# Where token operands begin in SBUF relative to the split weights: one encoder layer in fp32 pieces on one core

## The chip, the cores and the metric

The kernel runs on one NeuronCore of a Trainium2 chip. The metric is the device time of one execution in microseconds (us). The time before is the median of three runs; beside it stands one execution that was taken with the hardware profiler, whose rows are shown further down.

## The reference

One layer over 256 tokens of width 2048, in float32. What matters here are its matrix products: each takes all tokens against a large weight matrix.

```python
h = rmsnorm(x, norm_mix_pre[l])
z = h @ w_in[l]                                  # 2048 x 13312
conv_b, conv_c, conv_in, q, k, v, g_a, g_b = jnp.split(z, IN_OFFSETS, axis=-1)
y_a = short_conv_mixer(conv_b, conv_c, conv_in, conv_w[l], w_out_conv[l])   # ... @ w_out
...
y_b = block_gqa(q, k, v) @ w_out_attn[l]
...
mixed = (gate_a * y_a + gate_b * y_b) @ w_merge[l]
x = x + rmsnorm(mixed, norm_mix_post[l])
h = rmsnorm(x, norm_mlp_pre[l])
f = jnp.square(jax.nn.relu(h @ w_up[l])) @ w_down[l]
x = x + rmsnorm(f, norm_mlp_post[l])
```

## The kernel before

**Split products.** Every fp32 operand is split into a high and a low float32r part (`split`: ScalarE writes `hi`, VectorE writes `lo = src - hi`), and each product is three matmuls: high x high, high x low, low x high.

**Weights.** A projection is one block of 512 output columns by 2048 inputs. Its weights come by DMA into `raw`, 128 x 1024 at a time, and are split into `whi` and `wlo` (lines 75 and 76). One such pair of tiles is called a granule here: 256 of the 2048 inputs, so a projection has 8 granules. `weights` takes the tiles of the granules from a ring of four in the pool `wts`; once the mixing part is over (line 486) a second ring of four, `wts2`, is there, and granules then go four to `wts`, four to `wts2`, in turn (line 123). A projection after that point therefore has four granules of either ring, `wts` first.

**Two kinds of projection.**
- `linear_channels` (lines 161 to 200): the weights are stationary (loaded into the array, 128 columns at a time) and the tokens move, 256 columns each. 24 matmuls a granule, from lines 175, 179 and 182. Used by the convolution's three inputs (12 projections), both gates (8), `w_oc` (4), `w_oa` (4) and `w_up` except its first (15): 43 projections.
- `linear` (lines 133 to 159): the tokens are stationary and the weights move, 512 columns each. 12 matmuls a granule, from lines 145 to 147. Used by K, V and Q (6 projections), `w_mg` (4), the first of `w_up` (1) and `w_dn` (16): 27 projections.

**Token operands** are made by `pair`: 128 partitions x (2, 16, 256) float32r, the high parts in the first half. Three tags, each one place: A holds `hT` (the normalised input; it moves for the convolution and the gates and is stationary for K, V, Q), later `xr`, later `fT` (the hidden layer, stationary for `w_dn`); B holds `yT` (moves for `w_oc`), then `mT` (stationary for `w_mg`), later `facc`; C holds `oT` (moves for `w_oa`), then `x2T` (moves for `w_up`, stationary for its first projection).

**Places.** Pools lie one behind the other in each partition in the order in which they are opened (lines 61 to 65, then `mx`, in whose place `wts2` and `late` are opened later), and each tile takes a multiple of 32 bytes. The tiles of `big`, `wts` and `wk` are all multiples of 256 bytes, so where `big` begins decides where all of them begin modulo 256. The small tiles of `sm` lie between `wk` and what follows.

**Order.** The three matmuls of a step follow each other without a pause; `later` and `tick` put the attention's and the convolution's small work between granules by a fixed count.

Of the kernel before, what the change touches and what calls it, by code (L numbers as in the profile page):

```python
# [9 lines left out]
F32 = mybir.dt.float32  # L10
F32R = mybir.dt.float32r
# [4 lines left out]
P = 128  # L16
D = 2048
T = 256
NT = T // P
KT = D // P  # L20
# [12 lines left out]
def trunk_kernel(  # L33
# [16 lines left out]
    nc = tc.nc  # L50
# [8 lines left out]
    WARM = 9  # L59

    const = ctx.enter_context(tc.tile_pool(name="const", bufs=1))
    big = ctx.enter_context(tc.tile_pool(name="big", bufs=1))
    wts = ctx.enter_context(tc.tile_pool(name="wts", bufs=WB))
    wk = ctx.enter_context(tc.tile_pool(name="wk", bufs=2))
    sm = ctx.enter_context(tc.tile_pool(name="sm", bufs=2))
    ps_acc = ctx.enter_context(tc.tile_pool(name="ps_acc", bufs=4, space=bass.MemoryType.PSUM))
    ps_tr = ctx.enter_context(tc.tile_pool(name="ps_tr", bufs=2, space=bass.MemoryType.PSUM))
    ps_at = ctx.enter_context(tc.tile_pool(name="ps_at", bufs=2, space=bass.MemoryType.PSUM))
# [11 lines left out]
                lo, src, scale, hi.bitcast(F32), op0=ALU.mult, op1=ALU.subtract  # L80
            )

    def pair(tag):

        both = big.tile([P, 2, KT, T], F32R, tag=tag, name=tag)
        return both[:, 0], both[:, 1], both

# [43 lines left out]
    def linear(act, wv, done, k0=0, k1=KT, lag=0, ahead=None):  # L133

        ah, al, _ = act
        accs = [ps_acc.tile([P, CH], F32, name="acc") for _ in range(NT)]

        def step(t, k, wh, wl):  # L140
            ts_ = slice(t * P, (t + 1) * P)
            for g in range(KG):
                a = k - k0 + g
                first, last = a == 0, a == k1 - k0 - 1
                nc.tensor.matmul(accs[t], lhsT=ah[:, a, ts_], rhs=wh[:, g, :], start=first, stop=False)  # L145
                nc.tensor.matmul(accs[t], lhsT=ah[:, a, ts_], rhs=wl[:, g, :], start=False, stop=False)  # L146
                nc.tensor.matmul(accs[t], lhsT=al[:, a, ts_], rhs=wh[:, g, :], start=False, stop=last)  # L147
            if k + KG == k1:
                done(t, accs[t])

        behind = []
        for gran in weights(wv, k0, k1, ahead):
            behind.append(gran)
            step(0, *gran)
            if len(behind) > lag:
                step(1, *behind.pop(0))
            tick()
        for gran in behind:
            step(1, *gran)

    def linear_channels(act, wv, done):

        ah, al, _ = act
        accs = [ps_acc.tile([P, 2, T], F32, name="acc") for _ in range(CH // P // 2)]

        def step(c, k, wh, wl):
            cs = slice(c * P, (c + 1) * P)  # L170
            acc = accs[c // 2][:, c % 2, :]
            for g in range(KG):
                a = k + g

                nc.tensor.matmul(  # L175
                    acc, lhsT=wh[:, g, cs], rhs=ah[:, a, :], start=a == 0 and c % 2 == 0, stop=False,
                    skip_group_check=True,
                )
                nc.tensor.matmul(  # L179
                    acc, lhsT=wh[:, g, cs], rhs=al[:, a, :], start=False, stop=False, skip_group_check=True  # L180
                )
                nc.tensor.matmul(  # L182
                    acc, lhsT=wl[:, g, cs], rhs=ah[:, a, :], start=False, stop=a == KT - 1, skip_group_check=True
                )


        end = []
        for gran in weights(wv, 0, KT):
            if gran[0] >= KT - END * KG:
                end.append(gran)  # L190
            else:
                for c in range(CH // P):
                    step(c, *gran)
                tick()
        for c in range(0, CH // P, 2):
            for gran in end:
                step(c, *gran)
                step(c + 1, *gran)
            done(c, accs[c // 2])
            tick(END // 2)  # L200
# [57 lines left out]
        nc.scalar.activation(act, zero[:, :1], AF.Square)  # L258
    ident = const.tile([P, P], F32, name="ident")
    make_identity(nc, ident)  # L260
    mhalf = const.tile([P, 1], F32, name="mhalf")
    nc.vector.memset(mhalf, -0.5)
    ch = const.tile([P, 7, KT], F32, name="ch")
    nc.scalar.dma_start(ch, chan)
    g_pre, g_mlp, cw = ch[:, 0, :], ch[:, 1, :], ch[:, 2:5, :]
    g_bias = ch[:, 5:7, :]

    hT = pair("A")

    def first_operands(k, n):  # L270
        xt = mx.tile([P, KA, T], F32, tag="rope", bufs=4, name="xt")
# [1 line left out]
        for i in range(n):  # L273
            split(xt[:, i, :], hT[0][:, k + i, :], hT[1][:, k + i, :], scale=g_pre[:, k + i : k + i + 1])

    rstd = const.tile([P, NT], F32, name="rstd")
    norm_row = wk.tile([P, 2, T], F32, name="bias", bufs=1)
    xv = x.rearrange("(t p) d -> p t d", p=P)
    tabs = [mx.tile([P, 2, NT, HD], F32, name=f"tab{i}", bufs=1) for i in range(2)]

    def norm_in():

        ss0 = const.tile([P, NT, 4], F32, name="ss0")
        for j in range(4):
            xj = mx.tile([P, NT, CH], F32, tag="t4", bufs=4, name="xj")
            nc.sync.dma_start(xj, xv[:, :, j * CH : (j + 1) * CH])
            for t in range(NT):
                row_squares(ss0[:, t, j : j + 1], xj[:, t, :])
        total(rstd, ss0)
        along_rows(norm_row[:, 0, :], [rstd[:, t : t + 1] for t in range(NT)])  # L290
        nc.vector.tensor_tensor(norm_row[:, 1, :], norm_row[:, 0, :], norm_row[:, 0, :], op=ALU.mult)
# [78 lines left out]
        hT, w_in[C_V], lambda t, acc: split(acc, vh[:, t, :], vl[:, t, :], scale=rstd[:, t : t + 1])  # L370
    )

    oT = pair("C")
    yT = pair("B")

    def mm3(acc, a, b, first, last):
        nc.tensor.matmul(acc, lhsT=a[0], rhs=b[0], start=first, stop=False)  # L377
# [3 lines left out]
    def attention(j):  # L381
# [5 lines left out]
        def scores(hp, t, prob):  # L387
            ts_ = slice(t * P, (t + 1) * P)
            sc = ps_at.tile([P, 2, T], F32, name="at")
            for i in range(2):  # L390
                mm3(sc[:, i, :], (qh[:, hp + i, ts_], ql[:, hp + i, ts_]), (kh[:, j, :], kl[:, j, :]), True, True)
            nmax = sm.tile([P, 2], F32, name="nmax")
            nc.vector.tensor_reduce(nmax, sc, axis=AX.X, op=ALU.max, negate=True)
            pr = mx.tile([P, 2, T], F32, name="pr")
            den = sm.tile([P, 2], F32, name="den")
            for i in range(2):
                nc.scalar.activation(
                    pr[:, i, :], sc[:, i, :], AF.Exp, bias=nmax[:, i : i + 1], accum_out=den[:, i : i + 1]
                )
            rden = sm.tile([P, 2], F32, name="rden")  # L400
            nc.vector.reciprocal(rden, den)
            for i in range(2):
                nc.vector.tensor_scalar_mul(pr[:, i, :], pr[:, i, :], rden[:, i : i + 1])
            prob.append(pr)
# [102 lines left out]
    for j in range(4):  # L507
# [4 lines left out]
                nc.vector.tensor_tensor(m[:, j * 4 + c : j * 4 + c + 2, :], acc, g[:, c : c + 2, :], op=ALU.mult)  # L512

        linear_channels(yT, w_oc[j], done)
    mT = pair("B")
    for j in range(4):
        g = gate(C_GB, j, 1)
        def done(c, acc):
# [14 lines left out]
    rows1 = const.tile([P, 6], F32, name="rows1")  # L533

    def row_rsqrt(parts, t, at):
        s = sm.tile([P, 1], F32, name="s1")
        nc.vector.tensor_reduce(s, parts[:, t, :], axis=AX.X, op=ALU.add)
        r = rows1[:, at : at + 1]
        rsqrt_mean(r, s, D)
        return r  # L540


    ss1 = const.tile([P, NT, 4], F32, name="ss1")
    ss2 = const.tile([P, NT, 4], F32, name="ss2")
    xr = big.tile([P, 2, NT, D], F32, tag="A", name="xr")[:, 0]
    nc.scalar.dma_start(xr, xv)
    x2T = pair("C")
    rstd2 = [None] * NT
    mgs = []

# [79 lines left out]
    before = [None] * NT  # L630

    def finish(t, last):
        ms = sm.tile([P, 1], F32, name="ms3")
        nc.vector.scalar_tensor_tensor(ms, ss3[:, t, 3:4], 1.0 / D, before[t], op0=ALU.mult, op1=ALU.add)
        r = sm.tile([P, 1], F32, name="rs3")
        nc.gpsimd.tensor_tensor(r, ms, mhalf, op=ALU.pow)
        for c in range(4):
            js = slice(c * CH, (c + 1) * CH)
            f = facc[:, t, js] if c < 3 else last
            nc.vector.scalar_tensor_tensor(x2[:, t, js], f, r, x2[:, t, js], op0=ALU.mult, op1=ALU.add)  # L640
            nc.sync.dma_start(outv[:, t, js], x2[:, t, js])

    def down(q, j, fT):
        js = slice(j * CH, (j + 1) * CH)
        g = gain_row(4 + j) if q == 3 else None

        def done(t, acc):
            fj = facc[:, t, js]
            if q == 0:
                nc.scalar.copy(fj, acc)  # L650
                return
            nc.vector.tensor_tensor(fj, acc, fj, op=ALU.add)
            if q < 3:
                return
            row_squares(ss3[:, t, j : j + 1], fj)
            if j < 3:
                nc.vector.tensor_tensor(fj, fj, g, op=ALU.mult)
            else:
                last = wk.tile([P, CH], F32, tag="cc", bufs=CCB, name="cc")
                nc.vector.tensor_tensor(last, fj, g, op=ALU.mult)  # L660
                finish(t, last)
            if j == 2:
                s = sm.tile([P, 1], F32, name="s1")
                nc.vector.tensor_reduce(s, ss3[:, t, :3], axis=AX.X, op=ALU.add)
                before[t] = rows1[:, 4 + t : 5 + t]
                nc.vector.tensor_scalar(before[t], s, 1.0 / D, EPS, op0=ALU.mult, op1=ALU.add)

        linear(fT, w_dn[j], done, q * KT, (q + 1) * KT, lag=LAG if q == 3 and j == 3 else 0)

    for q in range(4):  # L670
        fT = pair("A")
        for j in range(4):
            if q == 0 and j == 0:
                hidden(q, j, fT)
# [65 lines left out]
```

## Time and profile before

| | |
|---|---|
| median of three runs | 1626.02 us (1625.46 to 1627.36) |
| the profiled execution | 1625.61 us |
| its span, first to last instruction | 1623.8 us |
| PE busy with matmuls | 1610.9 us, 99% of the span, 11210 instructions |
| weight loads (PEld) | 1497.9 us, 92% |
| VectorE, ScalarE, GpSimd busy | 947.5 us (58%), 709.5 us (44%), 35.6 us (2%) |
| DMA | 306.28 MB, mean 189 GB/s |

Busy time of PE counts matmuls that overlap in the pipeline, so how fast they follow each other is read from their starts, or from how many stand in a stretch of time. The span lacks the 1.8 us of the execution that lie around it.

### The profile page before, as it was taken

How to read it: one execution, taken by the hardware profiler on the slowest of the kernel's cores; microseconds unless marked ns; L12 is line 12 of the kernel's file. 1: busy time of each engine (PE TensorE's matmuls, PEld its weight loads, DVE VectorE, ACT ScalarE, POOL GpSimd, SP SyncE). 2: the span in 40 equal slices, each digit the busy share in tenths (PEclk: the TensorE clock that was granted, in tenths of full speed). 3: DMA queues.
4: the chain of work that ended last, by engine and by line, in shares of the span. 5: the costliest groups of instructions: out<-in, count | busy, mean ns of one | idle time of the engine just before them, and what ended most of it. 6: DMA issues, size and time to landing. Idle time of an engine off the chain costs nothing.

```text
span 1623.8 us, 26863 instructions
## 1 busy us (share of the span) xinstructions
PE 1610.9 (99%) x11210; PEld 1497.9 (92%) x11210; DVE 947.5 (58%) x1107; ACT 709.5 (44%) x860; POOL 35.6 (2%) x23
## 2 busy tenths in 40 slices
PE   9999999999999999999999999999999999999997
PEld 7899999999999999999988898889988998899986
DVE  6767676576764544555554865446654565555654
ACT  7444444444454443444444644444433344333441
POOL 0210101001000000000000000000000000000000
PEclk9999999999999999999999999999999999999999
DMA  8654545555475556565765566555565565556562
GB/s 317 204 177 156 181 147 181 181 167 183 149 241 186 186 188 194 186 190 184 243 204 177 172 209 195 189 187 189 185 197 189 187 190 189 193 182 195 191 200 83
DMA packets 86297, 306.28 MB, mean 189 GB/s; under 512 B 9632, under 2 KB 10016, under 8 KB 85920
## 3 DMA queue, kind: packets, MB, share of 16 engines
q1 hardware_dynamic: 84608, 300.32, 57.2%
q10 hardware_dynamic: 1568, 4.25, 0.8%
q8 instruction: 87, 1.43, 0.4%
q14 instruction: 34, 0.28, 0.1%
HBM read 302.44 MB, written 2.10 MB: 188 GB/s over the span
## 4 chain that ended last, share of the span: by engine, by line
PE 97%; DVE 1%; issue 1%; DMA 0%; POOL 0%; ACT 0%; SPq 0%; DVEq 0%; POOLq 0%; ACTq 0%
PE acc L182 20%; PE acc L175 20%; PE acc L179 20%; PE acc L146 12%; PE acc L147 12%; PE acc L145 12%; PE at L377 0%; PE at L379 0%; PE at L378 0%; PE tr L410 0%; DMA raw<-in_w_in 0%; PE tr L224 0%; POOL rs L236 0%; DVE wlo L76 0%; PE tr L575 0%
## 5 line engine op out<-in xcount | busy, mean ns | idle before, releaser
L76 DVE TENSOR_TENSOR wlo<-raw,whi 128x1024 fp32r<-128x1024 f32 (+1 forms) x561 | 684.2, 1221 | 602.8 <-ACT whi L75 590.9
L75 ACT CAST whi<-raw 128x1024 fp32r<-128x1024 f32 (+1 forms) x561 | 587.1, 1048 | 774.2 <-PE acc L179 401.6
L175 PE MATMUL acc<-A,whi 128*128 128x256 f32 x1280 | 362.3, 283 | 0.0
L182 PE MATMUL acc<-A,wlo 128*128 128x256 f32 x1280 | 360.4, 282 | 0.0
L179 PE MATMUL acc<-A,whi 128*128 128x256 f32 x1280 | 360.3, 282 | 0.0
L175 PE MATMUL acc<-C,whi 128*128 128x256 f32 x1216 | 340.0, 280 | 0.0
L182 PE MATMUL acc<-C,wlo 128*128 128x256 f32 x1216 | 339.9, 280 | 0.0
L179 PE MATMUL acc<-C,whi 128*128 128x256 f32 x1216 | 339.9, 279 | 0.0
L145 PE MATMUL acc<-whi,A 128*128 128x512 f32 x704 | 275.0, 392 | 2.2 <-ACT whi L75 2.2
L146 PE MATMUL acc<-wlo,A 128*128 128x512 f32 x704 | 275.9, 392 | 1.0 <-DVE wlo L76 1.0
L147 PE MATMUL acc<-whi,A 128*128 128x512 f32 x704 | 275.3, 391 | 0.0
L179 PEld LDWEIGHTS acc<-A,whi 128*128 128x128 f32 x1280 | 244.4, 191 | 0.2
L175 PEld LDWEIGHTS acc<-A,whi 128*128 128x128 f32 x1280 | 244.4, 191 | 0.2
L182 PEld LDWEIGHTS acc<-A,wlo 128*128 128x128 f32 x1280 | 244.5, 191 | 0.0
L175 PEld LDWEIGHTS acc<-C,whi 128*128 128x128 f32 x1216 | 230.8, 190 | 0.2
L179 PEld LDWEIGHTS acc<-C,whi 128*128 128x128 f32 x1216 | 230.8, 190 | 0.2
L182 PEld LDWEIGHTS acc<-C,wlo 128*128 128x128 f32 x1216 | 230.8, 190 | 0.0
L145 PEld LDWEIGHTS acc<-whi,A 128*128 128x128 f32 x704 | 131.8, 188 | 32.1 <-ACT whi L75 3.1
L146 PEld LDWEIGHTS acc<-wlo,A 128*128 128x128 f32 x704 | 132.0, 187 | 31.9 <-DVE wlo L76 2.7
L147 PEld LDWEIGHTS acc<-whi,A 128*128 128x128 f32 x704 | 132.0, 187 | 29.0
L182 PE MATMUL acc<-B,wlo 128*128 128x256 f32 x256 | 71.6, 280 | 0.0
L179 PE MATMUL acc<-B,whi 128*128 128x256 f32 x256 | 71.6, 280 | 0.0
(144 smaller groups left out, 1115.6 us busy)
## 6 DMA issues: line engine op xcount, KB each, us to landing
raw<-in_w_in SPq DMA_DIRECT2D x207, 512.0 KB, 4.3
raw<-in_w_up SPq DMA_DIRECT2D x128, 512.0 KB, 3.5
raw<-in_w_dn SPq DMA_DIRECT2D x128, 512.0 KB, 3.4
raw<-in_w_oc SPq DMA_DIRECT2D x32, 512.0 KB, 4.4
raw<-in_w_oa SPq DMA_DIRECT2D x32, 512.0 KB, 4.3
raw<-in_w_mg SPq DMA_DIRECT2D x32, 512.0 KB, 4.1
xj<-in_x SPq DMA_DIRECT2D x4, 512.0 KB, 9.0
xr<-in_x ACTq DMA_DIRECT2D x1, 2048.0 KB, 9.7
```

The lines of the kernel that those rows point to most:

```text
L75: nc.scalar.copy(hi, src)
L76: nc.vector.tensor_tensor(lo, src, hi.bitcast(F32), op=ALU.subtract)
L145: nc.tensor.matmul(accs[t], lhsT=ah[:, a, ts_], rhs=wh[:, g, :], start=first, stop=False)
L146: nc.tensor.matmul(accs[t], lhsT=ah[:, a, ts_], rhs=wl[:, g, :], start=False, stop=False)
L147: nc.tensor.matmul(accs[t], lhsT=al[:, a, ts_], rhs=wh[:, g, :], start=False, stop=last)
L175: nc.tensor.matmul(acc, lhsT=wh[:, g, cs], rhs=ah[:, a, :], start=a == 0 and c % 2 == 0, stop=False, skip_group_check=True,)
L179: nc.tensor.matmul(acc, lhsT=wh[:, g, cs], rhs=al[:, a, :], start=False, stop=False, skip_group_check=True)
L182: nc.tensor.matmul(acc, lhsT=wl[:, g, cs], rhs=ah[:, a, :], start=False, stop=a == KT - 1, skip_group_check=True)
```

## The change

The order of the instructions on every engine stays as it was, and so do their shapes; no matmul, copy or DMA is added or taken away. What changes is where tiles begin.

- The pool `sm` is opened directly behind `const`, ahead of `big`.
- Small tiles are put together or share a place (`ss0` and `ss1` in `ss01`; `mhalf` and `rstd` in `half`; `nmax` and `den` in `tops`; three late tiles take the tags of earlier ones). The memset of `mhalf` becomes one of 128 x 4.
- `pair` is told whether the tokens move or are stationary, and takes its part of a slightly longer tile: A is 64 bytes longer and begins 64 bytes in where tokens move; B is 192 bytes longer and begins 192 bytes in where they are stationary; C stays.

```diff
     const = ctx.enter_context(tc.tile_pool(name="const", bufs=1))
+
+    sm = ctx.enter_context(tc.tile_pool(name="sm", bufs=2))
     big = ctx.enter_context(tc.tile_pool(name="big", bufs=1))
     wts = ctx.enter_context(tc.tile_pool(name="wts", bufs=WB))
     wk = ctx.enter_context(tc.tile_pool(name="wk", bufs=2))
-    sm = ctx.enter_context(tc.tile_pool(name="sm", bufs=2))
...
-    def pair(tag):
-
-        both = big.tile([P, 2, KT, T], F32R, tag=tag, name=tag)
-        return both[:, 0], both[:, 1], both
+
+
+    LATE = {"A": {True: 16, False: 0}, "B": {True: 0, False: 48}, "C": {True: 0}}
+
+    def pair(tag, moving):
+
+        n, at = 2 * KT * T, LATE[tag][moving]
+        flat = big.tile([P, n + max(LATE[tag].values())], F32R, tag=tag, name=tag)
+        both = flat[:, at : at + n].rearrange("p (h k t) -> p h k t", h=2, k=KT)
+        return both[:, 0], both[:, 1]
...
-    mhalf = const.tile([P, 1], F32, name="mhalf")
-    nc.vector.memset(mhalf, -0.5)
+    ss01 = const.tile([P, 2, NT, 4], F32, name="ss01")
+    half = const.tile([P, 4], F32, name="half")
+    nc.vector.memset(half, -0.5)
+    mhalf = half[:, :1]
+    rstd = half[:, 2:4]
...
-    hT = pair("A")
+    hT = pair("A", True)
...
-    oT = pair("C")
-    yT = pair("B")
+    oT = pair("C", True)
+    yT = pair("B", True)
...
-    mT = pair("B")
+    mT = pair("B", False)
...
-    x2T = pair("C")
+    x2T = pair("C", True)
...
-        fT = pair("A")
+        fT = pair("A", False)
```

The byte at which the operands of the large products begin in each partition, and that byte modulo 256, as the two programs are built:

| tile | before | modulo 256 | after | modulo 256 |
|---|---|---|---|---|
| `wts` ring, first `whi` (the others at steps of 4096) | 148768 | 32 | 149440 | 192 |
| `wts2` ring, first `whi` (the others at steps of 4096) | 190432 | 224 | 190400 | 192 |
| A, moving (`hT`) | 17696 | 32 | 18176 | 0 |
| A, stationary (`fT`) | 17696 | 32 | 18112 | 192 |
| B, moving (`yT`) | 99616 | 32 | 100096 | 0 |
| B, stationary (`mT`) | 99616 | 32 | 100288 | 192 |
| C (`oT`, `x2T`) | 66848 | 32 | 67328 | 0 |
| `kv` (attention) | 50464 | 32 | 50944 | 0 |
| `qh`, `ph` (attention) | 212960, 190432 | 224 | 212928, 190400 | 192 |

## Rows read from the trace of the kernel before

**Rows 1.** The page: span and the engines' busy time.

```profile
span 1623.8 us, 26863 instructions
PE 1610.9 (99%) x11210; PEld 1497.9 (92%) x11210; DVE 947.5 (58%) x1107; ACT 709.5 (44%) x860; POOL 35.6 (2%) x23
```

**Rows 2.** The page: the chain that ended last, shares of the span by engine.

```profile
PE 97%; DVE 1%; issue 1%; DMA 0%; POOL 0%; ACT 0%; SPq 0%; DVEq 0%; POOLq 0%; ACTq 0%
```

**Rows 3.** Waits of PE, longest first: total us, times, longest us.

```profile
PE acc L145 <- ACT whi L75: 2.2, 2, 1.5
PE tr L256 <- DVE mhalf L262: 1.1, 1, 1.1
```

**Rows 4.** Windows of one w_up projection's two halves; counts include matmuls reaching in.

```profile
core 0: us, PE busy (x) PEld busy (x) DVE busy (x) ACT busy (x) POOL busy (x), PEclk, DMA share, GB/s
...
1103.66:1115.18 11.52, 11.52 (x98) 11.52 (x97) 8.16 (x9) 4.92 (x6) 0.00 (x0) 1.00 0.56 176
1115.18:1126.06 10.88, 10.88 (x98) 10.88 (x97) 5.21 (x6) 4.38 (x5) 0.00 (x0) 1.00 0.58 193
```

**Rows 5.** Timeline of PE where a w_up projection changes rings: start us, us.

```profile
1092.54 0.28 PE L179 MATMUL acc<-C,whi 128*128 128x256 f32 x1
1092.66 0.28 PE L182 MATMUL acc<-C,wlo 128*128 128x256 f32 x1
1092.78 0.28 PE L175 MATMUL acc<-C,whi 128*128 128x256 f32 x1
...
1093.12 0.28 PE L175 MATMUL acc<-C,whi 128*128 128x256 f32 x1
```

**Rows 6.** Windows of one w_dn projection's two halves.

```profile
1192.97:1203.87 10.90, 10.90 (x49) 9.01 (x48) 5.84 (x6) 4.21 (x4) 0.00 (x0) 1.00 0.60 194
1203.87:1215.07 11.20, 11.20 (x49) 8.98 (x48) 5.20 (x5) 4.19 (x4) 0.00 (x0) 1.00 0.58 187
```

**Rows 7.** Lines 182 and 145: ns min/median/max, first and last start.

```profile
L182 PEld LDWEIGHTS acc<-A,wlo x1280: 187/192/193, 76.7 to 786.6; 128*128 128x128 f32 x183
L182 PE MATMUL acc<-A,wlo x1280: 276/283/285, 76.8 to 786.7; 128*128 128x256 f32 x183
L182 PEld LDWEIGHTS acc<-C,wlo x1216: 187/188/192, 652.5 to 1526.6; 128*128 128x128 f32 x174
L182 PE MATMUL acc<-C,wlo x1216: 276/278/287, 652.6 to 1526.7; 128*128 128x256 f32 x174
...
L145 PE MATMUL acc<-whi,A x704: 388/389/507, 4.9 to 1614.6; 128*128 128x512 f32 x176
...
L145 PE MATMUL acc<-whi,B x128: 388/394/398, 809.2 to 899.0; 128*128 128x512 f32 x128
```

**Rows 8.** Line 378, the attention's products: scores, then values.

```profile
L378 PEld LDWEIGHTS at<-kv,qh x32: 187/188/188, 103.4 to 422.3; 128*128 128x128 f32 x32
L378 PE MATMUL at<-kv,qh x32: 276/276/276, 103.5 to 422.4; 128*128 128x256 f32 x32
L378 PEld LDWEIGHTS at<-pl,kv x32: 187/190/192, 116.7 to 436.1; 128*128 128x128 f32 x32
L378 PE MATMUL at<-pl,kv x32: 276/279/283, 116.8 to 436.2; 128*128 128x256 f32 x32
```

**Rows 9.** Timeline of PE in the convolution, ring wts alone.

```profile
190.55 0.28 PE L179 MATMUL acc<-A,whi 128*128 128x256 f32 x1
...
191.50 0.28 PE L175 MATMUL acc<-A,whi 128*128 128x256 f32 x1
```

**Rows 10.** Window of Q projection granules, ring wts, and of a convolution with attention.

```profile
62.12:67.56 5.44, 5.44 (x26) 4.50 (x24) 3.12 (x3) 2.11 (x2) 0.00 (x0) 1.00 0.88 315
130.00:140.00 10.00, 10.00 (x87) 10.00 (x86) 10.00 (x20) 4.16 (x6) 0.00 (x0) 1.00 0.29 91
```

**Rows 11.** Timeline there: a granule's low part on DVE.

```profile
134.24 1.22 DVE L76 TENSOR_TENSOR wlo<-raw,whi 128x1024 fp32r<-128x1024 f32 x1
```

**Rows 12.** Timeline there: PE's first use of that low part.

```profile
136.09 0.28 PE L182 MATMUL acc<-A,wlo 128*128 128x256 f32 x1
```

More of the change, by code (lines that the diff above doesn't have):

```diff
@@ L133, in linear @@
     def linear(act, wv, done, k0=0, k1=KT, lag=0, ahead=None):
-        ah, al, _ = act
+        ah, al = act
         accs = [ps_acc.tile([P, CH], F32, name="acc") for _ in range(NT)]
@@ L161, in linear_channels @@
     def linear_channels(act, wv, done):
-        ah, al, _ = act
+        ah, al = act
         accs = [ps_acc.tile([P, 2, T], F32, name="acc") for _ in range(CH // P // 2)]
@@ L274, in first_operands @@
             split(xt[:, i, :], hT[0][:, k + i, :], hT[1][:, k + i, :], scale=g_pre[:, k + i : k + i + 1])
-    rstd = const.tile([P, NT], F32, name="rstd")
     norm_row = wk.tile([P, 2, T], F32, name="bias", bufs=1)
@@ L281, in norm_in @@
     def norm_in():
-        ss0 = const.tile([P, NT, 4], F32, name="ss0")
+        ss0 = ss01[:, 0]
         for j in range(4):
@@ L391, in scores @@
                 mm3(sc[:, i, :], (qh[:, hp + i, ts_], ql[:, hp + i, ts_]), (kh[:, j, :], kl[:, j, :]), True, True)
-            nmax = sm.tile([P, 2], F32, name="nmax")
+            tops = sm.tile([P, 2, 2], F32, name="tops")
+            nmax, den = tops[:, 0], tops[:, 1]
             nc.vector.tensor_reduce(nmax, sc, axis=AX.X, op=ALU.max, negate=True)
             pr = mx.tile([P, 2, T], F32, name="pr")
-            den = sm.tile([P, 2], F32, name="den")
             for i in range(2):
@@ L535, in row_rsqrt @@
     def row_rsqrt(parts, t, at):
-        s = sm.tile([P, 1], F32, name="s1")
+        s = sm.tile([P, 1], F32, tag="rden", name="s1")
         nc.vector.tensor_reduce(s, parts[:, t, :], axis=AX.X, op=ALU.add)
@@ L540, in row_rsqrt @@
         return r
-    ss1 = const.tile([P, NT, 4], F32, name="ss1")
+    ss1 = ss01[:, 1]
     ss2 = const.tile([P, NT, 4], F32, name="ss2")
@@ L632, in finish @@
     def finish(t, last):
-        ms = sm.tile([P, 1], F32, name="ms3")
+        ms = sm.tile([P, 1], F32, tag="ms", name="ms3")
         nc.vector.scalar_tensor_tensor(ms, ss3[:, t, 3:4], 1.0 / D, before[t], op0=ALU.mult, op1=ALU.add)
-        r = sm.tile([P, 1], F32, name="rs3")
+        r = sm.tile([P, 1], F32, tag="rs", name="rs3")
         nc.gpsimd.tensor_tensor(r, ms, mhalf, op=ALU.pow)
@@ L662, in done @@
             if j == 2:
-                s = sm.tile([P, 1], F32, name="s1")
+                s = sm.tile([P, 1], F32, tag="rden", name="s1")
                 nc.vector.tensor_reduce(s, ss3[:, t, :3], axis=AX.X, op=ALU.add)
```

## The prediction, made blind

> **What bounds the kernel now.** First the page: PE is busy 1610.9 of 1623.8 us, and the chain that ended last is PE for 97% of the span [rows 1, 2]. Then PE's own waits: the two longest entries come to 2.2 and 1.1 us in total [rows 3]. So the time is how fast matmuls follow each other, and the other engines count only where they would fall behind. VectorE is busy 58%, ScalarE 44% [rows 1]. The granted clock is 1.00 in every window that I cite, which is the 2.4 GHz level [rows 4, 6, 10].
>
> Busy time says nothing of the pace, so I went on to windows cut where a projection changes rings. A `w_up` projection (tokens move, 256 columns) takes 11.52 us for its four `wts` granules and 10.88 us for its four `wts2` granules [rows 4]. Both hold 96 matmuls, 4 x 24; the counts of 98 include two that reach in. That is 120.0 and 113.3 ns each. The timeline shows the step: the starts lie 0.12 us apart up to 1092.78, and the next three intervals take 0.34 us together [rows 5]. The projections with stationary tokens show a step of the other sign: 10.90 us on `wts`, 11.20 us on `wts2`, for 48 matmuls, so 227.1 and 233.3 ns [rows 6].
>
> The trace of before is thus already an experiment on the change. Its tokens all begin at 32 modulo 256, `wts` at 32 and `wts2` at 224. Counted as moving minus stationary modulo 256, the halves are at 0 and at 64 where tokens move, and at 0 and at 192 where weights move. The durations show where the loss sits. For moving tokens in A, four fifths of whose granules are in `wts`, the median matmul is 283 ns and its weight load 192 ns; the least are 276 and 187 [rows 7]. For moving weights the common value is 388 to 389 ns and the slower one 394 [rows 7]. Per column the better halves agree: 113.3 ns for 256 and 227.1 ns for 512 are both 0.443 ns. So I read 0 as costing about 7 ns when 256 columns move and nothing when 512 do, and 64 as costing nothing when 256 columns move.
>
> The attention is a third witness, outside the two rings. Its scores move `kv` (32) over stationary `qh` (224), distance 64, and all 32 matmuls of line 378 take exactly 276 ns. Its values move `pl` (224) over `kv` (32), distance 192, and spread from 276 to 283 [rows 8]. So 64 is clean there too, and 192 is not.
>
> **The change, part by part.**
>
> *Moving tokens.* After the change they begin at 0 and all weights at 192, in both rings: distance 64 everywhere. Granules now at 0 are the 12 convolution projections whole, 96, since only `wts` exists then, and four in each of the 31 later ones, 124: 220 granules. The convolution has the slow pace too: eight intervals in 0.95 us [rows 9]. Four granules save 11.52 - 10.88 = 0.64 us [rows 4], so 55 x 0.64 = **35.2 us gained**. The `wts2` halves are there already and gain nothing.
>
> *Stationary tokens with a place of their own* (`mT` for `w_mg`, `fT` for `w_dn`, 20 projections) go to distance 0 in all granules. Their 80 `wts2` granules save 0.30 us for four [rows 6]: 20 x 0.30 = **6.0 us gained**.
>
> *Stationary tokens that must serve both ways.* `hT` for K, V and Q and `x2T` for the first `w_up` stay where moving tokens are, so there the weights move at distance 192. K, V and Q run at the good pace now: 24 matmuls in 5.44 us, 226.7 ns [rows 10]. 48 granules of theirs and four of `w_up` go from the good to the poor price: 13 x 0.30 = **3.9 us lost**. Part of this can hide at the very start, where PE waits for the first splits anyway [rows 3]; that is at most the eight granules of K, 0.6 us, and I leave it out.
>
> *The rest.* Merged small tiles and the longer memset add no instruction. Small tiles that share a place could add a wait, but they are a few bytes of work on VectorE and GpSimd, 42% and 98% idle. The attention keeps its distances, 64 for scores and 192 for values. All this I take as nothing; the cover is that PE waits for almost none of it [rows 3].
>
> *What a faster PE could uncover.* It consumes a granule of moving tokens in 2.72 instead of 2.88 us. In the later stages the `wts2` halves already run so, with DMA at a share of 0.58 and VectorE busy 5.21 of 10.88 us [rows 4]. The tight place is a convolution with attention: VectorE is busy for 10.00 of 10 us [rows 10], a low part ends at 134.24 + 1.22 = 135.46 [rows 11], and PE takes it at 136.09 [rows 12]: 0.63 us to spare. In such a stretch PE would come up to 10 x 0.16 / 2.88 = 0.56 us sooner, just within it. If all of that became a wait at each of the four attention blocks, it would cost 2.2 us. I take nothing, and keep 2.2 for the range.
>
> Sum: 35.2 + 6.0 - 3.9 = 37.3 us. From the profiled execution's 1625.6 us that leaves 1588.3; the median of the runs is 0.4 us above that execution, so I say **1588.7 us**. What is late next is still PE, at the clean pace throughout.
>
> The Trainium skill speaks against this. SBUF — State Buffer, Who interferes with whom, says that PE's moving operand and its weight load have independent read ports and that PE and ACT never wait on anyone. By that, distance could not matter, and the sum would be 0 instead of 37.3 us; it is rival 1 below that would hold. The trace disagrees at least in this: the same matmul of the same stage takes 120.0 or 113.3 ns by the half of the projection alone.
>
> **The rivals.**
>
> 1. *The halves differ by something other than distance*, for instance by which part of the partition the ring lies in, and the change does nothing: **1626**. For: the two rings do lie apart (148,768 onward, 190,432 onward), and the scores' stationary `qh` lies high as `wts2` does. Against: the sign turns round with the role. A place that is slow to read should not be the poor one as stationary weights and the good one as moving weights; distance also has to change its sense with the width, though, so this is not a proof.
>
> 2. *The place of the weights alone counts, and 192 behaves like 32* rather than like 224. Then every granule of moving tokens goes at 0.120 us a matmul: the 124 `wts2` granules lose 31 x 0.64 = 19.8 us, and the 84 stationary `wts2` granules gain 21 x 0.30 = 6.3. That is 13.5 us slower, **1639.5**. It decides itself on one figure: the interval in a `w_up` projection's second half. For it: nothing before stands at 192. Against: the argument in rival 1.
>
> 3. *The period is 512 bytes, not 256.* Slices of tokens and weights move by multiples of 512 bytes, and the pace within a window is steady, so 512 is safe. But `fT` (18112) and the rings (149440) lie an odd multiple of 256 apart, which no row shows. Bounds: 10.90 and 11.20 us for four granules [rows 6]. At 11.20, `w_dn`'s 64 `wts2` granules gain nothing and its 64 `wts` granules lose: 16 x 0.30 twice, 9.6 us back, **1598.3**.
>
> 4. *Starting at a multiple of 64 bytes helps by itself.* All large operands before stand at 32 modulo 64, all after at 0, so no row prices it. At the 2.4 GHz level 256 columns would be 106.7 ns against the clean 113.3. If all of that vanished, 344 granules at 24 x 6.6 ns and 216 at 12 x 13.8 ns would give back another 54 and 36 us: 1498 at the far end. I name half, **1544**, and hold it unlikely, since the clean price is the same 0.443 ns per column in both shapes.
>
> TensorE: Matmul & The Clock Gate, Back-to-back issue gap, in the Trainium skill, gives N / 2.4 + 2.5 ns, 109.2 for 256 columns and 215.8 for 512. No row here is that short. An estimate from that page for all 10,848 large matmuls would be another 63 us off, near rival 4.
>
> **How the numbers follow.** Forecast 0.78, with its own range of 1584 to 1594: the 0.64 and 0.30 us are read to 0.02, which is 1.5 us on the sum, the feed adds up to 2.2, the start takes off up to 0.6, and the rest is for runs that differ. Rival 3 gets 0.08, rival 4 0.05, rival 1 0.05, rival 2 0.04. A measurement of this kernel can tell about 0.2%, 3.3 us, from no change. Faster: 0.78 + 0.08 + 0.05 = 0.91; same 0.05; slower 0.04. The range runs from 1582 to 1599, so that it takes in rival 3 and leaves out 1, 2 and 4.
>
> **What the profile after would show.** A `w_up` projection: two halves of 10.88 us, and line 182 on A and C with a median of 276 and loads of 187 to 188. A `w_dn` projection: two halves of 10.90. Q granules: four in 11.20 instead of 10.88. PE's waits still a few us, none on `wlo` in the convolution. The prediction is wrong if the halves still differ (rival 1), if both stand at 11.52 (rival 2), if `w_dn` alone stands at 11.20 (rival 3), or if 256 columns take less than 113 ns (rival 4).

## The result, and the profile after

The changed kernel takes **1608.88 us** (median, 1607.96 to 1609.13) against 1626.56 for the kernel before in the same comparison: a ratio of 0.9891 [0.9874, 0.9908]. The gain is 17.7 us. 37.3 were forecast, and the range ended at 1599. The direction was right and the size was not.

In the page of the kernel after, the first two lines and the shares of the chain answer to [rows 1, 2].

```profile
span 1607.0 us, 26865 instructions
PE 1594.8 (99%) x11210; PEld 1485.8 (92%) x11210; DVE 948.0 (59%) x1107; ACT 710.0 (44%) x860; POOL 35.7 (2%) x23
...
PE 98%; DVE 1%; DMA 0%; POOL 0%; issue 0%; ACT 0%; SPq 0%; DVEq 0%; POOLq 0%; ACTq 0%
```

The two largest waits of PE in the view of waits of the kernel after (total us, times, longest) answer to [rows 3].

```profile
PE acc L152 <- ACT whi L76: 1.7, 2, 1.2
PE tr L263 <- DVE half L270: 1.1, 1, 1.1
```

Nothing new waits, so the missing 19.6 us must lie in the pace of the matmuls. The forecast named the places to look: each half of a projection should take 10.88 us. The view of windows gives, for the kernel after, the two halves of a `w_up` projection (1088 and 1099), four granules of a gate (534) and the two halves of a `w_dn` projection (1000 and 1011). They answer to [rows 4, 6]; the columns are the same.

```profile
1088.52:1099.83 11.31, 11.31 (x98) 11.31 (x97) 8.11 (x9) 4.87 (x6) 0.00 (x0) 1.00 0.60 180
1099.83:1111.14 11.31, 11.31 (x99) 11.31 (x98) 5.28 (x6) 4.44 (x5) 0.00 (x0) 1.00 0.62 194
534.49:545.37 10.88, 10.88 (x99) 10.88 (x97) 6.50 (x6) 4.22 (x4) 0.00 (x0) 1.00 0.60 183
1000.63:1011.51 10.88, 10.88 (x50) 9.01 (x48) 4.90 (x4) 4.70 (x5) 0.00 (x0) 1.00 0.66 195
1011.51:1022.39 10.88, 10.88 (x50) 9.01 (x48) 4.90 (x4) 4.81 (x5) 0.00 (x0) 1.00 0.66 194
```

Gates and `w_dn` do what was forecast: 96 matmuls of 113.3 ns, and 48 of 226.7. `w_up` doesn't. Both its halves take 11.31 us, 117.8 ns a matmul, a price that stood in neither half before (120.0 and 113.3). Yet `w_up` and `w_oa` read their moving tokens from the very same bytes (`x2T` and `oT` share tag C), with stationary weights at the same place modulo 256 and in code that is the same. The view of one line, the third matmul of the three, shows it by operand (duration as least/median/most):

```profile
L189 PEld LDWEIGHTS acc<-A,wlo x1280: 187/188/188, 79.0 to 773.6; 128*128 128x128 f32 x183
L189 PE MATMUL acc<-A,wlo x1280: 276/276/283, 79.1 to 773.7; 128*128 128x256 f32 x183
L189 PEld LDWEIGHTS acc<-C,wlo x1216: 187/188/189, 643.4 to 1511.2; 128*128 128x128 f32 x174
L189 PE MATMUL acc<-C,wlo x1216: 276/279/284, 643.5 to 1511.3; 128*128 128x256 f32 x174
```

On C, which here is `w_oa` and `w_up` together, the median is 279 ns, not 276. The loads are back at 188 on A and C, where A had 192 before [rows 7]. So the third price is neither the poor one of before (283 with loads of 192) nor the good one. I call the three paces **locked** (120.0 ns, loads 192), **poor** (117.8, loads 188) and **clean** (113.3, loads 188).

**Where the time went, stage by stage.** These windows hold the same work in both kernels; of before first, then of after: the second convolution with attention, the 15 projections from the second gate to the last `w_oa`, the second quarter of `w_up` (768 matmuls), and the start with K, V and Q.

```profile
175.60:252.80 77.20, 77.20 (x649) 77.20 (x648) 54.40 (x86) 35.51 (x52) 5.64 (x2) 1.00 0.52 165
473.20:809.20 336.00, 336.00 (x2882) 336.00 (x2881) 173.14 (x164) 142.79 (x160) 0.00 (x0) 1.00 0.62 197
1081.30:1170.90 89.60, 89.60 (x770) 89.60 (x769) 50.37 (x52) 37.09 (x40) 0.00 (x0) 1.00 0.58 188
4.90:76.60 71.70, 68.48 (x303) 54.81 (x303) 52.27 (x84) 43.54 (x65) 8.23 (x3) 1.00 0.78 273
```

```profile
176.70:252.00 75.30, 75.30 (x650) 75.26 (x650) 54.37 (x86) 35.42 (x52) 5.64 (x2) 1.00 0.53 168
469.20:795.60 326.40, 326.40 (x2882) 326.40 (x2881) 173.27 (x164) 143.57 (x160) 0.00 (x0) 1.00 0.64 203
1065.90:1156.40 90.50, 90.50 (x770) 90.49 (x769) 50.46 (x52) 37.16 (x40) 0.00 (x0) 1.00 0.62 187
4.90:78.90 74.00, 71.56 (x303) 56.28 (x303) 52.30 (x84) 43.12 (x65) 8.23 (x3) 0.98 0.75 266
```

Taken from the start of a stage's first matmul to that of the next stage's, in the two profiled executions:

| stage | forecast gain | measured gain |
|---|---|---|
| gates after the first, `w_oc`, `w_oa` (15 projections) | 9.6 | 9.6 |
| `w_up` (15 projections) | 9.6 | -3.3 |
| convolutions, with the first gate | 16.0 | 8.1 |
| `w_mg` and `w_dn` | 6.0 | 6.6 |
| K, V, Q and the first `w_up` | -3.9 | -4.2 |
| sum | 37.3 | 16.8 (spans: 16.8) |

Two stages hold the error: `w_up`, 12.9 us short, which is its 30 stretches of four granules at 11.31 - 10.88 = 0.43 us, and the convolutions, 7.9 us short. The other differences are 0.6 us and less.

### The profile page after: what moved, and what is told of

Its sections match the earlier page's. It is cut to its first block, busy times and chain, and to the rows that moved or that the text cites. A ratio compares the mean times of both kernels' runs of the same rounds, so it can differ in the third digit from the quotient of the medians.

```text
span 1607.0 us, 26865 instructions
## 1 busy us (share of the span) xinstructions
PE 1594.8 (99%) x11210; PEld 1485.8 (92%) x11210; DVE 948.0 (59%) x1107; ACT 710.0 (44%) x860; POOL 35.7 (2%) x23
## 4 chain that ended last, share of the span: by engine, by line
PE 98%; DVE 1%; DMA 0%; POOL 0%; issue 0%; ACT 0%; SPq 0%; DVEq 0%; POOLq 0%; ACTq 0%
PE acc L182 20%; PE acc L189 20%; PE acc L186 20%; PE acc L153 12%; PE acc L154 12%; PE acc L152 12%; PE at L386 0%; PE at L387 0%; PE at L388 0%; PE tr L419 0%; DMA raw<-in_w_in 0%; PE tr L231 0%; POOL rs L243 0%; DVE wlo L77 0%; PE tr L584 0%
## 5 line engine op out<-in xcount | busy, mean ns | idle before, releaser
L182 PE MATMUL acc<-A,whi 128*128 128x256 f32 x1280 | 357.1, 279 | 0.0
L186 PE MATMUL acc<-A,whi 128*128 128x256 f32 x1280 | 355.2, 278 | 0.0
L189 PE MATMUL acc<-A,wlo 128*128 128x256 f32 x1280 | 355.1, 277 | 0.0
L186 PEld LDWEIGHTS acc<-A,whi 128*128 128x128 f32 x1280 | 240.4, 188 | 0.2
L182 PEld LDWEIGHTS acc<-A,whi 128*128 128x128 f32 x1280 | 240.3, 188 | 0.2
L189 PEld LDWEIGHTS acc<-A,wlo 128*128 128x128 f32 x1280 | 240.1, 188 | 0.0
L182 PEld LDWEIGHTS acc<-C,whi 128*128 128x128 f32 x1216 | 228.1, 188 | 0.2
L186 PEld LDWEIGHTS acc<-C,whi 128*128 128x128 f32 x1216 | 227.8, 187 | 0.2
L182 PE MATMUL acc<-B,whi 128*128 128x256 f32 x256 | 70.7, 276 | 0.0
L186 PE MATMUL acc<-B,whi 128*128 128x256 f32 x256 | 70.7, 276 | 0.0
```

Of the source, the lines that this page charges most:

```text
L182: nc.tensor.matmul(acc, lhsT=wh[:, g, cs], rhs=ah[:, a, :], start=a == 0 and c % 2 == 0, stop=False, skip_group_check=True,)
L186: nc.tensor.matmul(acc, lhsT=wh[:, g, cs], rhs=al[:, a, :], start=False, stop=False, skip_group_check=True)
L189: nc.tensor.matmul(acc, lhsT=wl[:, g, cs], rhs=ah[:, a, :], start=False, stop=a == KT - 1, skip_group_check=True)
```

## The experiments

The expectations call the theories by letters. **P**: at distance 64 there are two self-sustaining paces, and the one that runs is inherited from what ran before. **A**: the absolute place counts. **K**: any extra matmuls at the head of a stage change its pace. **S**: the stage itself decides. **H**: the clean pace is handed on from the locked one where the stationary side changes its place. A stroke marks the same theory as sharpened by the runs before it. In the diffs, - is the changed kernel. Nothing of the computation is left out in any run; the extra matmuls of some write into sums that the first real matmul clears.

**All operands 32 bytes on** (`shift32`): weights at 224, tokens at 32 modulo 256, every distance as in the changed kernel.

```diff
+    pad = const.tile([P, 8], F32, name="pad")
+    nc.vector.memset(pad, 0.0)
     sm = ctx.enter_context(tc.tile_pool(name="sm", bufs=2))
```

> The changed kernel with 32 bytes more ahead of all operands: every distance stays, but the places return to 32 and 224 modulo 256 (tokens that move at 32, weights at 224), where the rows of before saw the clean 113.3 ns. Theory P (two paces): at distance 64 there are two steady paces, 113.3 and about 117.8 ns, and what ran just before decides which; the absolute place does not matter. Then w_up (15 projections) stays near 117.8 ns and the time near 1609 us (1606 to 1612). Theory A (absolute place): places at multiples of 64 bytes bring the second pace; back at 32 and 224 every matmul with 256 moving columns takes 113.3 ns, and the time falls to about 1589 us.

Measured: 1608.55 us, 0.9893 [0.9878, 0.9907]. Four granules of `w_up`, then of a gate, in its windows:

```profile
1087.41:1098.71 11.30, 11.30 (x98) 11.30 (x97) 8.10 (x9) 4.85 (x6) 0.00 (x0) 1.00 0.59 185
533.37:544.25 10.88, 10.88 (x98) 10.88 (x97) 6.50 (x6) 4.22 (x4) 0.00 (x0) 1.00 0.62 197
```

The same as after, with stationary weights at 224 as in the clean second half of before. A falls: the absolute places don't count. Rival 4 of the prediction falls with it, since tokens and weights now begin at 32 modulo 64 and nothing is lost.

**Six extra matmuls ahead of the first `w_up` projection with moving tokens of each quarter**: in `kick6` weights on weights (distance 0), in `kick6_ctrl` tokens on weights (distance 64).

```diff
+            for _ in range(kick if gran[0] == 0 else 0):
+                nc.tensor.matmul(
+                    accs[0][:, 0, :], lhsT=gran[1][:, 0, :P], rhs=gran[1][:, 0, :T], start=True, stop=False,
+                    skip_group_check=True,
+                )
...
-        linear_channels(x2T, w_up[q * 4 + j], done)
+        linear_channels(x2T, w_up[q * 4 + j], done, kick=6 if (q == 0 and j == 1) or (q > 0 and j == 0) else 0)
```

> The changed kernel with six extra matmuls ahead of the first w_up projection with moving tokens of each of the four quarters (24 in all): stationary weights, and 256 columns of the same weight tile moving, distance 0; their sums are cleared by the first real matmul. Theory P: at distance 0 the stream falls into one fixed rhythm, and from that it enters distance 64 at the clean pace, as at each change of rings before; w_up then runs at 113.3 ns throughout: 2880 matmuls x 4.5 ns = 13.0 us gained, 24 x 0.12 = 2.9 us paid, about 1599 us. Theory A: nothing in w_up changes (117.8 ns), 2.9 us slower, about 1612 us.

> The same 24 extra matmuls, but with 256 columns of the tokens moving, so at distance 64: the pause and the number of matmuls are those of the run with distance 0, the distance is not. Theory P: w_up stays near 117.8 ns, about 1612 us. If it were the extra matmuls at the start and not their distance that set the rhythm (theory K), w_up would be at 113.3 ns here too, about 1599 us. Theory A: about 1612 us.

Measured: 1610.35 us, 0.9904 [0.9887, 0.992], and 1610.41 us, 0.9904 [0.9889, 0.9919]. In `kick6`, by the view of the line, the loads of the extra matmuls, and by its windows the four granules behind one kick:

```profile
L197 PEld LDWEIGHTS acc<-whi x24: 187/188/193, 908.4 to 1422.1; 128*128 128x128 f32 x24
```

```profile
1065.97:1077.30 11.33, 11.33 (x99) 11.33 (x98) 4.90 (x4) 4.10 (x5) 0.00 (x0) 1.00 0.56 183
```

The kick came to the loads of the locked pace (191 to 193 ns) in three of the four quarters, not in the first (190), and `w_up` stayed poor in all. K falls, and P as I had put it missed. Two things differ from the ring change of before [rows 5]: there the stationary side changes its place, here the moving side does; and there 96 matmuls had run at distance 0, here six.

**Tokens on tokens** (`kickw`): the same kick with `lhsT=ah[:, 1, :P], rhs=ah[:, 0, :]`, so that at its end the stationary side moves on to the weights; 6, 3, 2 and 1 of them in the four quarters.

> The changed kernel with extra matmuls ahead of the first w_up projection with moving tokens of each quarter: 6, 3, 2 and 1 in the four quarters. Both operands are x2T, so the distance is 0 as in the run with moving weights, but here the tokens move already and it is the stationary operand that changes place when the real work begins, as at each change of rings before. Theory H (hand-over): distance 64 has two paces, 113.3 and 117.8 ns, and the clean one is entered when the weight load moves away by 64 bytes under a stream that goes on at its place. Then w_up runs at 113.3 ns after the kicks that are long enough: with all four 2880 x 4.5 ns = 13.0 us gained, 1.4 paid, 1597 us; with the six alone 2.6 gained in the first quarter, about 1608 us. Theory S (the stage): w_up has its pace of 117.8 ns whatever ran before, from something in the stage, such as the writes of ScalarE and VectorE beside it; about 1610 us.

Measured: 1608.64 us, 0.9892 [0.9875, 0.9908]. Six of them worked for a while. Below are the kick's loads from the view of the line, then the windows of 48 matmuls right behind the six and of 96 matmuls later in that quarter, behind its transposes:

```profile
L197 PEld LDWEIGHTS acc<-C x12: 187/188/192, 910.6 to 1422.5; 128*128 128x128 f32 x12
```

```profile
911.53:916.96 5.43, 5.43 (x50) 5.43 (x49) 3.50 (x4) 2.88 (x4) 0.00 (x0) 1.00 0.87 311
920.60:932.00 11.40, 11.40 (x100) 11.40 (x99) 6.59 (x6) 4.68 (x5) 0.00 (x0) 1.00 0.79 266
```

5.43 us for 48 is 113.1 ns: clean. The transposes ended it. Three, two and one did nothing. This is the first sign for H, and shows that a small interruption, here four transposes, is enough to lose the pace. The time says nothing of it: it is near the 1608 us that H named for the six alone, but H meant 2.6 us gained, and 48 matmuls at the clean pace are 0.2.

**The same behind the transposes, and 5 and 4 of them elsewhere** (`kickb`): 6 in the third projection of the first quarter, then 6, 5 and 4 at the heads of the others.

> The changed kernel with extra matmuls of x2T on x2T (distance 0) where w_up's tokens begin to move after the last transposes of the first quarter (6), and at the head of the other three quarters (6, 5 and 4). The run with 6, 3, 2 and 1 showed the clean pace after the 6 alone, and only until the next transposes. Theory H (hand-over, two paces): w_up runs at 113.3 ns from the third projection on, and stays there without further help: (384 + 3 x 768) x 4.5 ns = 12.1 us gained, 21 x 0.12 = 2.5 paid, 1599 us; if 5 and 4 are too few, those quarters give nothing, 1605 to 1606 us. Theory S (the stage sets the pace): w_up falls back to 117.8 ns within a projection, about 1611 us.

Measured: 1610.92 us, 0.9901 [0.9884, 0.9917]; no kick had an effect.

```profile
L197 PEld LDWEIGHTS acc<-C x21: 187/188/189, 931.7 to 1421.5; 128*128 128x128 f32 x21
```

No load exceeded 189 ns: these kicks never reached the locked pace, so they don't test the hand-over. Six matmuls are too few to reach it reliably.

**All tokens at one other distance** (`u128`, `u96`, `u32`, `u192`): `LATE` all 0, and a gap behind `yT` of 256 bytes less the distance. The edit for 192:

```diff
-    LATE = {"A": {True: 16, False: 0}, "B": {True: 0, False: 48}, "C": {True: 0}}
+    LATE = {t: {True: 0, False: 0} for t in "ABC"}
...
+    gap = big.tile([P, 16], F32, tag="gap", name="gap")
+    nc.vector.memset(gap, 0.0)
```

> The changed kernel with all token operands at one place, 128 bytes from the weights modulo 256, whether they move or are stationary. No row shows this distance. Theory P asks only that a distance has steady paces of its own; bounds by the nearest rows are 113.3 and 120.0 ns for 256 columns and 227.1 and 233.3 ns for 512. If 128, the farthest from 0, is free of loss for both, the time is about 1587 us; if it behaves like 0 for 256 columns and like 192 for 512, about 1650 us. Theory A says nothing on it beyond the same bounds.

> All token operands at one place, 96 bytes past the weights, moving or stationary (so weights that move are at 160). Theory H says that 64 is near an edge, since it has two paces; further off, at 96, the clean pace should hold in w_up and in the convolution, 113.3 ns for 256 columns, and 512 columns pay 227 to 234 ns: 1588 to 1603 us. If the loss only grows with distance from 64, as the 119 ns at 128 lets one think, 256 columns take 114 to 119 ns: 1600 to 1645 us.

> All token operands at one place, 32 bytes past the weights, moving or stationary (weights that move are at 224). Between 0 (120.0 ns) and 64 (113.3 or 117.8 ns) for 256 columns and between 192 (233.3 ns) and 0 (227.1 ns) for 512. Theory H: 256 columns near 120 ns, as the start of the weight load falls into the same stretch as at 0: about 1640 us. Theory S says only the bounds: 1588 to 1660 us.

> All token operands at one place, 192 bytes past the weights, moving or stationary (weights that move are at 64). For 256 columns the nearest rows are the attention's values at 192, 113 to 122 ns, mean 117; for 512 columns nothing was seen at 64, bounds 227.1 to 240 ns. Theory H: two or more paces again, 1600 to 1640 us. Theory S: w_up differs from the gates at the same places.

Measured, four granules in us (one run each; where weights move, the distance is 256 less the one in the first column):

| distance of moving tokens | total | gate | `w_up` | `w_dn` |
|---|---|---|---|---|
| 32 | 1628.30 | 11.20 | 11.20 | 11.20 |
| 96 | 1657.57 | 11.51 | 11.51 | 11.24 |
| 128 | 1644.56 | 11.39 | 11.52 | 11.15 |
| 192 | 1612.49 | 11.31 | 10.88 | 10.99 |

Two expectations missed. At 96, H had the clean pace hold (1588 to 1603 us, and 1645 was the upper end otherwise), and it is the slowest; at 32, H named about 1640 us. For 192 the windows of a gate and of `w_up` stand below:

```profile
535.17:546.48 11.31, 11.31 (x99) 11.31 (x97) 6.42 (x6) 4.21 (x4) 0.00 (x0) 1.00 0.61 185
1099.07:1109.95 10.88, 10.88 (x99) 10.88 (x97) 8.16 (x9) 4.92 (x6) 0.00 (x0) 1.00 0.61 177
```

That is the changed kernel turned round: the gates poor and `w_up` clean, so 192 has the same two paces as 64. S as first put, by which `w_up` is slow whatever its operands' places, falls. S as expected for this run, that gates and `w_up` differ at one distance, came true: a pace fixed by stage and distance together is still open here. No distance tried is clean throughout; 64 and 192 alone reach 113.3 ns.

**A distance for each stage** (`hybrid`, `hybrid2`): since gates were clean at 64 and `w_up` at 192, `hT` and `oT` at 64 and `x2T` at 192; `yT` at 192 in `hybrid` and, in `hybrid2`, where B is placed ahead of C, at 64 with its neighbours. A merged small tile and a gap of 64 bytes set the base. Both share these lines:

```diff
-    LATE = {"A": {True: 16, False: 0}, "B": {True: 0, False: 48}, "C": {True: 0}}
+    LATE = {"A": {True: 32, False: 0}, "B": {True: 0, False: 0}, "C": {True: 0, False: 32}}
...
-    x2T = pair("C", True)
+    x2T = pair("C", False)
```

> The changed kernel with other places and no extra matmul: hT and oT move at 64 as in the change, x2T at 192, yT at 192; fT and mT stand so that the weights that move beside them are at 64. In the run with all tokens at 192 w_up went at 113.4 ns and w_dn at 228.9. Theory H: w_up again enters the clean pace from w_dn's rhythm, 2880 x 4.4 ns = 12.7 us gained; w_dn and w_mg go at 228.9 instead of 226.8 ns, 1920 x 2.1 = 4.0 us lost; w_oc at 192 between gates at 64 lies between 113.3 and 117.8 ns, 0 to 3.5 us lost: 1600 to 1604 us. Theory S: the pace belongs to the place, 192 in w_up alone, and the sum is the same; the two differ in w_oc, where S sees 117.8 ns as in the run at 192 and H the clean pace of the gates carried over.

Measured: 1608.46 us, 0.9884 [0.9869, 0.9898], above the 1600 to 1604 expected. `w_up` is clean as hoped, but the gates behind the first `w_oc`, at the same 64 as in the changed kernel, are poor. The windows are of four granules each: of the first gate, the first `w_oc`, the second `w_oc`, the third gate and `w_up`.

```profile
456.55:467.43 10.88, 10.88 (x98) 10.88 (x97) 7.29 (x7) 6.57 (x7) 0.00 (x0) 1.00 0.83 297
467.43:478.74 11.31, 11.31 (x98) 11.31 (x97) 6.73 (x6) 6.62 (x9) 0.00 (x0) 1.00 0.70 247
512.66:523.55 10.89, 10.89 (x98) 10.89 (x97) 6.62 (x6) 5.13 (x6) 0.00 (x0) 1.00 0.57 186
534.43:545.74 11.31, 11.31 (x99) 11.31 (x97) 6.49 (x6) 4.19 (x4) 0.00 (x0) 1.00 0.60 188
1095.23:1106.11 10.88, 10.88 (x98) 10.88 (x97) 8.17 (x9) 4.93 (x6) 0.00 (x0) 1.00 0.57 184
```

Here S falls also in its second form. At 64, the first gate is clean and the others poor; at 192, the first `w_oc`, behind a clean gate, is poor, and the second, behind a poor one, is clean. Stage and distance are the same each time, and what ran before is not. The second `w_oc` also shows a clean pace that no locked stretch came before, so H is not the only way in.

> As the run with x2T at 192, but yT moves at 64 like the gates, and mT stands so that its weights are at 192. Theory H': gates, w_oc and w_oa hand one clean rhythm on to each other as in the change (113.3 ns), which the alternation of 64 and 192 in the last run broke (117.8 ns); w_up keeps 113.4 ns and w_dn 228.9. Against the change: w_up 2880 x 4.4 ns = 12.7 us gained, w_dn 1536 x 2.1 = 3.2 us and w_mg 384 x 6 = 2.3 us lost: about 1602 us. Theory S': gates stay at 117.8 ns as in the last run because of the other places around them: about 1611 us.

Measured: 1599.84 us (1599.63 to 1600.39), 0.9837 [0.9824, 0.9851]. With `hT`, `yT` and `oT` all at 64, the clean pace is back and is passed along:

```profile
532.68:543.56 10.88, 10.88 (x99) 10.88 (x97) 6.49 (x6) 4.21 (x4) 0.00 (x0) 1.00 0.64 191
1086.27:1097.15 10.88, 10.88 (x99) 10.88 (x97) 8.16 (x9) 4.93 (x6) 0.00 (x0) 1.00 0.64 188
```

**The ring change of before, put back for one granule** (`kickslot`): no matmul is added. In the first `w_up` projection of each quarter whose tokens move, the weights of the first `wts2` granule stand 64 bytes on. Its 24 matmuls are at distance 0, and behind them the stationary side moves back, as at the ring change of before.

```diff
+                if pool is not wts and slot == 0:
+                    at = 16 if kick else 0
+                    hi, lo = (
+                        pool.tile([P, KG * CH + 64], F32R, name=n, bufs=1)[:, at : at + KG * CH].rearrange(
...
-        linear_channels(x2T, w_up[q * 4 + j], done)
+        linear_channels(x2T, w_up[q * 4 + j], done, kick=j == (q == 0))
```

> The changed kernel, with no extra matmul: in the first w_up projection with moving tokens of each quarter, the fifth granule's weights stand 64 bytes on, at the tokens' own place (distance 0), for 24 matmuls; all other granules stay at 64. That repeats the change of rings of before once a quarter. Six extra matmuls were once enough and once not; the failures never reached the steady 120 ns with loads of 192 ns. Theory H' (hand-over from the locked rhythm of distance 0): 24 matmuls reach that rhythm, as they do at each ring change before, and what follows runs at 113.3 ns to the quarter's end: (456 + 3 x 648) x 4.5 ns = 10.8 us gained, 96 x 2.2 ns = 0.2 paid, about 1598 us. Theory S' (the clean pace after distance 0 needs a change of ring, or lasts only one projection): 1605 to 1609 us.

Measured: **1597.71 us** (1596.34 to 1599.08), 0.9824 [0.981, 0.9837], the best of all, 11.2 us below the changed kernel. The windows of one quarter follow each other in time: four granules ahead, the shifted granule, the other three of its half, and the next projection.

```profile
1062.01:1073.32 11.31, 11.31 (x98) 11.31 (x96) 4.90 (x4) 4.67 (x5) 0.00 (x0) 1.00 0.60 185
1073.32:1076.19 2.87, 2.87 (x26) 2.87 (x25) 1.23 (x1) 1.05 (x1) 0.00 (x0) 1.00 0.62 183
1076.19:1084.35 8.16, 8.16 (x74) 8.16 (x73) 4.02 (x5) 3.38 (x4) 0.00 (x0) 1.00 0.65 194
1084.35:1095.23 10.88, 10.88 (x98) 10.88 (x97) 8.17 (x9) 4.93 (x6) 0.00 (x0) 1.00 0.59 182
1095.23:1106.11 10.88, 10.88 (x98) 10.88 (x97) 5.21 (x6) 4.38 (x5) 0.00 (x0) 1.00 0.65 202
```

Poor (117.8 ns), locked for 24 matmuls (119.6), then clean (8.16 us for 72 is 113.3) for the rest of the quarter. The halves before and behind the kick have the same places and the same code; only what ran before them differs. All four quarters do this, and `w_up` as a whole gets back 10.5 of the missing 12.9 us; the rest lies in the halves ahead of the kicks and in the kicks. That is the cause of the missing 12.9 us, shown both ways at 64: with the locked stretch of before put back the clean pace comes back, and without one `w_up` stays poor. No run moved the granule to a distance other than 0, so it isn't shown that the stretch must be a locked one, nor, since `kick6` differs in length too, that it must be the stationary side that moves on.

## Why the prediction was wrong

**The bound** was right: PE at its pace, with nothing else late. The uncovered waits for which 2.2 us were kept in the range did not come; the largest waits of PE are still 1.7 and 1.1 us.

**Moving tokens (35.2 us) is the term that failed**: it measured 9.6 - 3.3 + 8.1 = 14.4. The step is the sentence that reads "64 as costing nothing when 256 columns move". Every row behind it, the `wts2` halves [rows 4, 5], had been entered from a locked `wts` half at distance 0, by a change of the stationary side. That entry was part of the observation, and the change removes it. Taking the locked halves away (a gain of 0.64 - 0.43 = 0.21 us for each) made the clean halves poor (a loss of 0.43), so `w_up` as a whole lost 15 times 0.22 us. The third witness, the attention's scores, was a coincidence of the same kind: before they took 276 ns at least and at most [rows 8], and after, at the same distance 64, they spread:

```profile
L387 PE MATMUL at<-kv,qh x32: 276/279/280, 105.3 to 420.2; 128*128 128x256 f32 x32
```

The other half of that reading, that 192 is not clean, failed too: in `u192` and `hybrid`, `w_up` at 192 takes 10.88 us for four granules.

That gates, `w_oc` and `w_oa` gained what was forecast is luck: a clean pace, reached in the fourth convolution near 434 us, runs on through all of them, and the forecast knew of no such condition. The windows stand right ahead of the last six products of the attention's values (23 matmuls from start to start) and right behind them (24):

```profile
430.44:433.15 2.71, 2.71 (x25) 2.71 (x24) 2.71 (x5) 0.59 (x1) 0.00 (x0) 1.00 0.61 184
433.85:436.57 2.72, 2.72 (x27) 2.72 (x25) 2.64 (x5) 1.54 (x2) 0.00 (x0) 1.00 0.84 256
```

That is 117.8 and 113.3 ns, and all four convolutions turn so behind their last values. Each begins poor, behind Q, and both times that four transposes met the clean pace, it was poor behind them. So only about 850 of the 2496 matmuls of this stage are clean, counted by the starts, where about 100 were before. That the values, at distance 192, bring the clean pace was read from the order of events in the trace, and not tried. Where scores follow the values at once, the pace turned from poor to clean twice and from clean to poor twice.

**Stationary tokens (6.0 us)** measured 6.6; distance 0 is clean at 512 columns.

**The loss of 3.9 us** measured 4.2, and that it comes so near is in part luck. The three later Q projections lost 1.8 us, as forecast, and the first `w_up` 0.1 of 0.3. The start with K, V and the first Q lost 2.3 us where 1.8 were forecast, but there the granted clock of this execution fell to the lower level, 1.2 GHz, behind two waits of PE of 1.21 and 0.53 us; before had waits there too, and no fall. Of before, then of after:

```profile
12.00:15.40 3.40, 3.40 (x16) 2.78 (x16) 3.38 (x6) 3.12 (x7) 0.00 (x0) 1.00 1.04 409
12.00:15.40 3.40, 3.40 (x10) 2.62 (x9) 3.36 (x6) 3.13 (x7) 0.00 (x0) 0.50 1.04 410
```

In the profiles of `shift32`, `kick6`, `kick6_ctrl`, `kickb` and `kickslot`, which have the same distances there and no such fall, the start takes 72.2 to 73.0 us against 71.7 before and 74.0 after: a loss of 0.6 to 1.3 us.

**Rivals.** Rival 1 (no effect) fell: both kinds of projection changed their pace where distance changed. Its premise holds in part, since the second halves of `w_up` kept their distance of 64 and went from 10.88 to 11.31 us. Here the Trainium skill, SBUF — State Buffer, Who interferes with whom, by which moving operand and weight load have independent ports and PE waits on no one, stands against the same 96 matmuls in 11.52, 11.31 and 10.88 us; the measurement decides. Rival 2 fell: no half stands at 11.52. Rival 3 fell: `w_dn` at 10.88 in both rings, with `fT` an odd multiple of 256 away. Rival 4 fell: nothing is under 113 ns. The true case, that a state outlives the places, was among none of them. It could have been suspected from the trace: the halves of before were the only rows at 64 that carried the sum, and all had the same predecessor.

## What to carry to other kernels

A price that is read from a stretch which always follows the same stretch belongs to the pair, not to the place alone. Before costing a change by it, look for a row where the same operands follow something else; if there is none, keep the other price in the range. Where matmuls bound a kernel, count matmuls per window at each change of stage, and compare stages that share operands: 11.31 against 10.88 us on the same bytes is the sign that history counts.

## What the runs showed of the hardware

- The pace of fp32r matmuls with a weight load each depends on how far the moving operand begins behind the stationary one modulo 256 bytes; moving all operands on by 32 bytes changed nothing (1608.55 against 1608.88 us). 256 columns, in ns: 120.0 at 0, 116.7 at 32, 119.9 at 96, 118.6 to 120.0 at 128. 512 columns, in ns: 227 at 0, 229 at 64, 232 at 128, 234 at 160, 233 at 192 and 224.
- At 64 and at 192, 256 columns have two paces, 113.3 and 117.8 ns, and either one keeps itself up over hundreds of matmuls. A 120-ns stretch of 24 matmuls, left by a change of the stationary side, brings the clean pace (`kickslot`); it also came behind the attention's values (after) and in `w_oc` at 192 behind poor gates at 64 (`hybrid`). Four transposes (`kickw`) or a stage of 512 columns (Q, in after) can end it.
- What stays open: what in the chip tells the two paces apart, why six extra matmuls that ended with a change of the moving side did nothing, whether a shift to another distance than 0 would do in `kickslot`, and why `w_up` at 192 is clean behind the same stages of moving weights that leave it poor at 64. Bringing the clean pace to the convolutions, about 8 us, was not tried.
